# Limiting how far the projection products may run ahead of the score chunks in the PE order of a hybrid encoder kernel

## The chip, the cores and the metric

The kernel runs on one core of a Trainium2 chip. Its metric is the device time of one launch in microseconds (us): the median of repeated executions. One more execution was recorded by the hardware profiler; all views of the profile speak of that one. The engines are named as in the profile: PE (TensorE, matrix products), PEld (its weight loads), DVE (VectorE), ACT (ScalarE), POOL (GpSimd) and SP (SyncE, which here only issues DMAs).

## The reference

Two layers of a bidirectional encoder over 2048 tokens of width 1024. Each layer normalises its input, projects it to the queries, keys, values and gates of four head groups (A: dense attention; B: windowed attention with sinks; C: neighbourhood attention; D: differential attention), joins the four gated outputs and projects back. Cut to what matters here:

```python
for l in range(DEPTH):                       # DEPTH = 2
    h = _rmsnorm(x, norm_g[l])
    z = jnp.einsum('bsd,de->bse', h, w_in[l])          # 1024 -> 3328 columns
    (q_a, k_a, v_a, g_a, q_b, k_b, v_b, g_b,
     q_c, k_c, v_c, g_c, q_d, k_d, v_d, g_d) = jnp.split(z, offs, axis=-1)
    ...
    # group D: 4 query heads, two score maps each, over all 2048 keys
    sc = jnp.einsum('bqkgcd,bskcd->cbkgqs', qi, k).astype(jnp.float32) * scale
    p = jax.nn.softmax(sc, axis=-1)
    w = (p[0] - lam * p[1]).astype(v.dtype)
    o = jnp.einsum('bkgqs,bskd->bqkgd', w, v)
    ...
    x = x + jnp.einsum('bsm,md->bsd', mix, w_out[l])
return _rmsnorm(x, final_g)
```

## The kernel before

A layer has four stages: the D columns are projected (with the transposes of x); then the attention of group D runs while the projections of A, B and C are done in its gaps; then the attention of A runs, with that of B and of C in between; at last the output projection. Precision is kept by splitting each operand of a projection into a high and a low part, so one product of the reference is three matmuls here (lines 320, 322 and 324, `in_proj_k`). The change concerns the second stage, called the D stage below.

**The D stage.** It has 32 units: 2 key heads times 16 tiles of 128 queries. A unit has 16 score chunks. A chunk is a matmul to a PSUM tile S of 128x512 (line 497); DVE copies it to the SBUF tile P and takes its row maximum (line 498). The pool of S has three buffers. After four chunks ACT takes the exponential over 2048 columns (line 505), and after eight DVE combines the two score maps (`comb`, line 724). Then come the unit's 32 transposes of P (tile PTp, line 514, evacuated by ACT at line 475), and the 16 value products (tile O, line 521; the profile shows two records for each). The output of a unit is normalised by a chain that goes through several engines, `fin_d`: the sums of squares by PE (tile fin, line 591), small DVE operations (lines 594, 595, 112), a power on POOL (line 114), DVE again (line 597), the gate on POOL (gg, line 545), and a transpose by PE (fin, line 550).

**The fillers.** The projections of A, B and C are 160 chunks of 24 products each, 3840 products a layer, written as a generator (`filler`) that gives one product of 128x256 at each step. `drive` writes the program of the D stage: it steps through the score chunks, and after each of them `fillers(n)` takes the next products from the generator. A unit has ten slots (two in `gap`, eight fronts), and each slot brings FR2 products. What is left when the first unit of A begins is written in one piece (`switch`).

**What sets the order.** In the D stage the order in which PE, DVE, ACT, POOL and SP issue is not the order in which the program is written. A scheduler goes through the program with a timing model of its own and gives each engine, at each point, the first instruction in program order whose inputs are ready in that model. A product whose score chunk would have to wait is therefore pulled ahead of the chunk. The engines then issue strictly in that order and wait on semaphores. In the stage of A the PE order is the written one (`manual_schedule`).

Of the kernel before, what the change touches and what calls it, by code (L numbers as in the profile page):

```python
# [31 lines left out]
WPT = 13  # L32
WOU = 360
KA0 = 16
FR2 = 11.2
SC64 = 64.0 ** -0.5
SC32 = 32.0 ** -0.5
NEG = -1e30
# [35 lines left out]
def trunk_kernel(ctx, tc, x, norm_g, w_in, w_out, qn_a, kn_a, sink_b, rpb_c, lam_q1, lam_k1, lam_q2, lam_k2,  # L74
                 subln_d, final_g, rope, bmask, out, depth=DEPTH):
    nc = tc.nc
    V, A, G, PE = nc.vector, nc.scalar, nc.gpsimd, nc.tensor
# [181 lines left out]
    for l in range(depth):  # L259
# [93 lines left out]
        with tc.tile_pool(name="wd", bufs=16, reuse_waits="tile") as wp, tc.tile_pool(name="st", bufs=3, reuse_waits="tile") as st:  # L353
# [84 lines left out]
            for t in range(NT):  # L438
                h = hs.pop(t)
                if t == WPT:  # L440
                    wb = big.tile([128, 4, 2, 256], F32R, tag="b", name="wb")
                    for k in range(4):
                        s = st.tile([128, 384], F32, tag="st", name="wst")
# [19 lines left out]
        with tc.tile_pool(name="sm", bufs=6, reuse_waits="tile") as sm, \  # L463
                tc.tile_pool(name="ov", bufs=2, reuse_waits="tile") as ov, tc.tile_pool(name="pp", bufs=2, reuse_waits="tile") as pp, \
                tc.tile_pool(name="sps", bufs=3, space=PSUM, reuse_waits="tile") as sps, tc.tile_pool(name="ops", bufs=1, space=PSUM, reuse_waits="tile") as ops, \
                tc.tile_pool(name="tps2", bufs=2, space=PSUM, reuse_waits="tile") as tps:
            later = []
            vt, kt = {}, {}
            tpool = cycle([tps])

# [9 lines left out]
            def tick():  # L480
                for e in list(later):
                    e[0] -= 1
                    if e[0] <= 0:
                        later.remove(e)
                        e[1]()
# [5 lines left out]
            def dense_scores(q_list, k_ap, scale, nscale, zacc, p):  # L491
                mx = sm.tile([128, 4], F32, tag="mx", name="mx")
                for j in range(4):
                    s = sps.tile([128, 512], F32, tag="s", name="S")
                    c = j * 512
                    for i, q in enumerate(q_list):
                        PE.matmul(s, lhsT=q, rhs=k_ap[:, c:c + 512], start=(i == 0), stop=(i == len(q_list) - 1))  # L497
                    V.tensor_scalar(p[:, c:c + 512], s, 1.0, None, op0=ALU.mult, op1=ALU.max, accum_out=mx[:, j:j + 1])  # L498
                    tick()
                    if j < 3:  # L500
                        yield
                nm = sm.tile([128, 1], F32, tag="nm", name="nm")
                jk = sm.tile([128, 4], F32, tag="jk", name="jk")
                V.tensor_scalar(jk, mx, nscale, None, op0=ALU.mult, op1=ALU.min, accum_out=nm)  # L504
                A.activation(p, p, ACTF.Exp, bias=nm, scale=scale, accum_out=zacc)  # L505
# [114 lines left out]
            def adv(g, n):  # L620
                for _ in range(n):
                    next(g, None)
# [3 lines left out]
            def drive(groups, fill, f_rate, extra):  # L626
# [17 lines left out]
                def fillers(n):  # L644
                    nonlocal fa
                    fa += n
                    k = int(fa)
                    fa -= k
                    adv(fill, k)

                def fin_all():
                    for f in list(fins):
# [3 lines left out]
                def slot(target):  # L656
                    fin_all()
                    n = max(0, math.ceil(target - 1e-6) - cnt[0])
                    for _ in range(n):
                        next(sg, None)  # L660
                        fillers(f_rate / n)
                    if n == 0:
                        fillers(f_rate)

                while cnt[0] < ends[0]:
                    next(sg)
                    fillers(f_rate / 2)
                for k, g in enumerate(groups):
# [8 lines left out]
                    i = 0  # L677
# [50 lines left out]
            if True:  # L728
# [180 lines left out]
                fill = filler()  # L909
# [70 lines left out]
            def a_scores(u):  # L980
                kv, t = u["kv"], u["t"]
                u["pre"]()
                qh, qlo = u["q"]()
                u["g"] = load_gate("A", t, kv)
                zt = sm.tile([128, 2], F32, tag="zt", name="zt")
                u["p"] = pp.tile([128, 2, S], F32, tag="p", name="P")
                for g in range(2):
                    yield from dense_scores([qh[g], qlo[g]], kt["A"][kv], rr_a[:, t, kv * 2 + g:kv * 2 + g + 1],
                                            nrr_a[:, t, kv * 2 + g:kv * 2 + g + 1], zt[:, g:g + 1], u["p"][:, g, :])
                    if g == 0:  # L990
                        yield
                u["rz"] = half_recip(zt)
                yield
# [112 lines left out]
            if True:  # L1106
# [75 lines left out]
                first["s"] = a_first  # L1182
                drive(units_d + [units[i:i + 3] for i in range(0, len(units), 3)], fill, FR2, ex3)
                ph3.close()
# [39 lines left out]
```

## Time and profile before

| What | us |
|---|---|
| median of three runs | 3577.78 |
| lowest and highest of them | 3574.85 and 3580.77 |
| the profiled execution, whole | 3572.38 |
| its span, from first to last instruction | 3570.6 |
| PE busy | 3432.0 |
| DVE busy | 2491.9 |
| ACT busy | 2109.9 |

The profiled execution is 5.4 us below the median, and 1.8 us of it lie outside the span. Of the views used below, the groups give for one line and operation the busy time, the mean duration and the idle time ahead of it; the table by stretches gives, for each stretch of the span (start and end in us, then its length), the busy time and the number of instructions of each engine and the TensorE clock granted; the waits give for whom an engine waited, in total, how often, and the longest; the timeline gives the start, the duration and the instruction. The busy time of PE is modelled: a matmul counts until its modelled end, so a PE that is busy may still be far from its highest rate.

### The profile page before, as it was taken

The numbers are of one execution on the slowest core, as the hardware profiler recorded it, in microseconds if no ns is written. First come the engines' busy times: TensorE is split into PE (matmuls) and PEld (weight loads), VectorE is DVE, ScalarE is ACT, GpSimd is POOL, SyncE is SP. The second block draws the span as 40 slices with busy tenths as digits, with TensorE's granted clock in tenths as the row PEclk, the third lists the DMA queues.
The fourth block names the chain that finished last, engine by engine and source line by source line (L and its number), as shares of the span: only waits on it lengthen the run. The fifth ranks groups of instructions, "written<-read, shape, count | busy, mean of one in ns | idle before, by whom it ended". The sixth has DMA issues, their size and how long they took to land.

```text
span 3570.6 us, 71576 instructions
## 1 busy us (share of the span) xinstructions
PE 3432.0 (96%) x25232; PEld 2964.9 (83%) x25232; DVE 2491.9 (70%) x7827; ACT 2109.9 (59%) x3963; POOL 963.4 (27%) x1604
## 2 busy tenths in 40 slices
PE   8989999999989999999999999999999899899999
PEld 8979889898967777878899888988888678678787
DVE  4387877878878887773234877787778688777733
ACT  4455656556667877771144555665566678777711
POOL 4455432552210001001044553345421000010000
PEclk9999999999999999999999999999999999999999
DMA  4532235323232345335445323252322333543243
GB/s 147 186 107 87 79 80 168 93 83 88 68 101 80 89 115 138 90 101 177 143 137 178 89 79 89 77 177 84 88 79 62 103 85 84 137 115 98 90 159 112
DMA packets 355777, 387.47 MB, mean 109 GB/s; under 512 B 59802, under 2 KB 298586, under 8 KB 350298
## 3 DMA queue, kind: packets, MB, share of 16 engines
q1 hardware_dynamic: 351098, 367.17, 34.8%
q10 hardware_dynamic: 4320, 15.73, 1.3%
q8 instruction: 199, 3.26, 0.4%
q14 instruction: 160, 1.31, 0.1%
HBM read 258.83 MB, written 123.91 MB: 107 GB/s over the span
## 4 chain that ended last, share of the span: by engine, by line
PE 78%; DVE 9%; DMA 4%; ACT 3%; POOL 3%; issue 2%; SPq 1%; DVEq 0%; POOLq 0%; ACTq 0%
PE O L521 11%; PE S L497 10%; PE PTp L514 10%; PE y L218 10%; PE z L320 9%; PE z L324 9%; PE z L322 9%; DVE P L498 4%; PE Obc L540 2%; PE PTp L532 2%; PE Sc L1044 1%; ACT P L505 1%; DMA wst<-in_w_in_dram 1%; DVE wt L314 1%; DVE P L724 1%
## 5 line engine op out<-in xcount | busy, mean ns | idle before, releaser
L498 DVE TENSOR_SCALAR_CACHE_REDUCE P<-S 128x512 f32<-128x512 f32 x1536 | 1025.4, 686 | 260.3 <-PE S L497 205.2
L320 PE MATMUL z<-wt,ht 128*128 128x256 f32 (+1 forms) x3008 | 892.7, 298 | 16.8 <-POOL wt L313 5.5
L322 PE MATMUL z<-wt,ht 128*128 128x256 f32 (+1 forms) x3008 | 887.0, 295 | 0.5 <-DVE wt L314 0.2
L324 PE MATMUL z<-wt,ht 128*128 128x256 f32 (+1 forms) x3008 | 883.1, 294 | 0.0
L514 PE MATMUL PTp<-idr,P 128*128 128x128 f32 x4096 | 630.7, 277 | 36.5 <-ACT P L475 18.2
L475 ACT COPY P<-PTp 128x512 f32<-128x512 f32 x896 | 513.3, 585 | 252.1 <-PE PTp L514 246.8
L505 ACT ACTIVATE P<-P,nm 128x2048 f32<-128x2048 f32 x256 | 514.1, 2008 | 156.6 <-DVE jk L504 153.9
L514 PEld LDWEIGHTS PTp<-idr,P 128*128 128x128 f32 x4096 | 492.2, 143 | 135.8 <-ACT P L475 34.2
L320 PEld LDWEIGHTS z<-wt,ht 128*128 128x128 f32 x3008 | 569.6, 190 | 37.7 <-POOL wt L313 7.3
L322 PEld LDWEIGHTS z<-wt,ht 128*128 128x128 f32 x3008 | 570.7, 190 | 12.5 <-DVE wt L314 2.2
L324 PEld LDWEIGHTS z<-wt,ht 128*128 128x128 f32 x3008 | 570.3, 190 | 9.2 <-issue 1.5
L497 PE MATMUL S<-kA,q 128*128 128x512 f32 x1024 | 361.9, 436 | 0.1
L218 PE MATMUL y<-wot,ms 128*128 128x512 f32 x1440 | 330.8, 392 | 0.0
L218 PEld LDWEIGHTS y<-wot,ms 128*128 128x128 f32 x1440 | 270.8, 188 | 59.7
L545 POOL TENSOR_TENSOR gg<-gt,rzh 128x128 f32<-128x128 f32 x192 | 76.7, 400 | 886.7 <-DVE rzh L606 324.5
L313 POOL TENSOR_SCALAR wt<-wst,g 128x256 fp32r<-128x256 f32 (+1 forms) x336 | 221.0, 669 | 333.3 <-PE z L324 222.1
L724 DVE SCALAR_TENSOR_TENSOR P<-P,cf,P 128x2048 f32<-128x2048 f32 x128 | 307.3, 2401 | 2.2
L505 ACT ACTIVATE P<-P,nm,rr_a 128x2048 f32<-128x2048 f32 x128 | 268.7, 2099 | 62.2 <-DVE jk L504 59.6
L521 PE MATMUL O<-P,vd 128*64 128x256 f32 x2048 | 238.5, 384 | 7.3 <-ACT P L475 7.3
L521 PE MATMUL O<-P,vA 128*64 128x256 f32 x2048 | 235.1, 382 | 0.0
L497 PE MATMUL S<-kd,qd 128*128 128x512 f32 x512 | 209.9, 428 | 9.2 <-DVE P L498 7.6
L497 PE MATMUL S<-kdt,qd 128*128 128x512 f32 x512 | 210.1, 436 | 8.4 <-DVE P L498 5.5
(195 smaller groups left out, 5103.0 us busy)
## 6 DMA issues: line engine op xcount, KB each, us to landing
wst<-in_w_in_dram SPq DMA_DIRECT2D x320, 128.0 KB
qd<-qd SPq DMA_DIRECT2D x128, 128.0 KB
htd<-ht SPq DMA_DIRECT2D x16, 1024.0 KB
ht<-htd SPq DMA_DIRECT2D x16, 1024.0 KB
q<-qsA SPq DMA_DIRECT2D x128, 128.0 KB
q<-qsB SPq DMA_DIRECT2D x64, 256.0 KB
q<-qc SPq DMA_DIRECT2D x64, 256.0 KB
mload<-mx ACTq DMA_DIRECT2D x30, 512.0 KB
```

Source lines behind the costliest of these rows:

```text
L218: PE.matmul(ys[c], lhsT=ms[:, a, kc], rhs=wts[k][:, b, c * 512:(c + 1) * 512], start=(k == 0 and i == 0), stop=(k == KD - 1 and i == 2))
L313: G.tensor_scalar(wt[:, 0, :], s, g8[:, k:k + 1], 0.0, op0=ALU.mult, op1=ALU.add)
L320: PE.matmul(z, lhsT=h[:, 0, kc], rhs=wk[:, 0, :], start=(k == 0), stop=False)
L322: PE.matmul(z, lhsT=h[:, 0, kc], rhs=wk[:, 1, :], start=False, stop=False)
L324: PE.matmul(z, lhsT=h[:, 1, kc], rhs=wk[:, 0, :], start=False, stop=(k == KD - 1))
L475: A.copy(dst, src)
L497: PE.matmul(s, lhsT=q, rhs=k_ap[:, c:c + 512], start=(i == 0), stop=(i == len(q_list) - 1))
L498: V.tensor_scalar(p[:, c:c + 512], s, 1.0, None, op0=ALU.mult, op1=ALU.max, accum_out=mx[:, j:j + 1])
L505: A.activation(p, p, ACTF.Exp, bias=nm, scale=scale, accum_out=zacc)
L514: PE.transpose(tp[:, (h * 2 + a) * 128:(h * 2 + a + 1) * 128], p[:, h, j * 128:(j + 1) * 128], idn)
L521: PE.matmul(u["o"][a * 64:(a + 1) * 64, 0:256], lhsT=u["v"](0, j), rhs=u["p"][:, :, j * 128:(j + 1) * 128], start=(n < 2), stop=(n >= NT - 2))
L724: V.scalar_tensor_tensor(p0, p1, cf, p0, op0=ALU.mult, op1=ALU.add)
```

## The change

Two things change. FR2, the products written per slot, goes from 11.2 to 12.0: ten slots of 12 make 120 products a unit, so the 3840 products of a layer fill 32 units. And every product that `fillers` writes gets an edge to the score chunk sixteen chunks back in the program: the scheduler must place it behind that chunk on PE. The edge carries no semaphore; it only orders instructions of the same engine. Sixteen chunks are one unit.

```diff
-FR2 = 11.2
+FR2 = 12.0
+LAG = 16
...
             later = []
+            score_ins = []
...
-                        PE.matmul(s, lhsT=q, rhs=k_ap[:, c:c + 512], start=(i == 0), stop=(i == len(q_list) - 1))
+                        m = PE.matmul(s, lhsT=q, rhs=k_ap[:, c:c + 512], start=(i == 0), stop=(i == len(q_list) - 1))
+                    score_ins.append(m.ins)
...
                     fa += n
                     k = int(fa)
                     fa -= k
-                    adv(fill, k)
+                    if len(score_ins) > LAG:
+                        with tc.issue_after(score_ins[-1 - LAG]):
+                            adv(fill, k)
+                    else:
+                        adv(fill, k)
```

No instruction is added or removed on any engine: 22274 on PE, 5909 on DVE, 3306 on ACT, 1609 on POOL, 2489 on SP both times. Their order differs from the D stage of each layer on, in the same way in both layers; the PE order of the A stage and of what follows is the same. The lines of the changed kernel are one to seven higher.

Counted in the PE order, between the value products (O) of one unit and of the next stand these numbers of projection products, units 1 to 31 of a layer (the 214 ahead of unit 0's are the same in both):

| Units | before | now |
|---|---|---|
| 1 to 8 | 125 147 138 154 110 96 116 97 | 158 135 176 150 94 102 76 95 |
| 9 to 16 | 125 132 156 166 160 104 118 153 | 164 160 142 128 120 102 115 143 |
| 17 to 24 | 157 140 152 96 117 75 92 124 | 120 120 120 120 96 102 91 77 |
| 25 to 31 | 118 120 151 160 27 0 0 | 115 125 120 178 161 21 0 |

Three places show it. The first is PE behind the value products of unit 29 of the first layer, near the end of the D stage. S is a score chunk, PTp the transposes of P, fin the two steps of the output chain. Before:

```order
L521 MATMUL O<-P,vd 64x256 x16
L514 MATMUL PTp<-idr,P 128x128 x2
L497 MATMUL S<-kdt,qd 128x512 x3
L591 MATMUL fin<-bones,sq 128x2
L514 MATMUL PTp<-idr,P 128x128 x4
L497 MATMUL S<-kdt,qd 128x512 x3
L514 MATMUL PTp<-idr,P 128x128 x8
L497 MATMUL S<-kdt,qd 128x512 x6
L550 MATMUL fin<-idr,gg 128x128
L514 MATMUL PTp<-idr,P 128x128 x16
```

Now:

```order
L524 MATMUL O<-P,vd 64x256 x16
L517 MATMUL PTp<-idr,P 128x128 x2
L321 MATMUL z<-wt,ht_8612 128x256
L323 MATMUL z<-wt,ht_8612 128x256
L325 MATMUL z<-wt,ht_8612 128x256
```

Before, no product is left there (the last one stands 27 products behind the value products of unit 28); now the last 21 products of the layer follow, ahead of the next score chunk.

The second place is PE behind the value products of unit 17, in the middle of the stage. Before (25 products in all stand ahead of the next score chunk):

```order
L521 MATMUL O<-P,vd 64x256 x16
L514 MATMUL PTp<-idr,P 128x128 x2
L324 MATMUL z<-wt,ht_8689 128x256
L320 MATMUL z<-wt,ht_8689 128x256
L322 MATMUL z<-wt,ht_8689 128x256
```

Now:

```order
L524 MATMUL O<-P,vd 64x256 x16
L517 MATMUL PTp<-idr,P 128x128 x2
L499 MATMUL S<-kdt,qd 128x512
L321 MATMUL z<-wt,ht_8277 128x256
L323 MATMUL z<-wt,ht_8277 128x256
L325 MATMUL z<-wt,ht_8277 128x256
```

The score chunk now stands directly behind the transposes, with no product ahead of it; six products and the next chunk follow. The same stands behind the value products of seven units of a layer (12, 13 and 16 to 20); behind those of unit 4 one product and two transposes of queries stand ahead of it as well. Before it stood so only in the part with no products left.

The third place is DVE, in the output chain of unit 21, from the second small operation (line 595 before, 598 now) to the last (597 and 600). L498 and L501 are the evacuations of score chunks, L315 the splitting of projection weights, L778 and L507 small steps of other work. Before:

```order
L594 TENSOR_TENSOR s_11129<-fin,rz_10266 128x2
L595 TENSOR_TENSOR s_11129<-s_11129,rz_10266 128x2
L112 TENSOR_SCALAR dme<-s_11129 128x2
L498 TENSOR_SCALAR P_11074,mx<-S 128x512 x2
L498 TENSOR_SCALAR P,mx<-S 128x512
L597 TENSOR_TENSOR drs<-drs,rz_10266 128x2
```

Now:

```order
L598 TENSOR_TENSOR s_11421<-s_11421,rz_10617 128x2
L501 TENSOR_SCALAR P_11351,mx<-S 128x512
L501 TENSOR_SCALAR P,mx<-S 128x512
L315 SCALAR_TENSOR_TENSOR wt<-wst,g_95,wt 128x256 x2
L778 TENSOR_TENSOR qt<-qT,qt 128x2x128
L113 TENSOR_SCALAR dme<-s_11421 128x2
L315 SCALAR_TENSOR_TENSOR wt<-wst,g_95,wt 128x256
L507 TENSOR_SCALAR jk,nm<-mx 128x4
L501 TENSOR_SCALAR P,mx<-S 128x512
L315 SCALAR_TENSOR_TENSOR wt<-wst,g_95,wt 128x256
L501 TENSOR_SCALAR P,mx<-S 128x512 x2
L600 TENSOR_TENSOR drs<-drs,rz_10617 128x2
```

More DVE work now stands inside this chain; one weight split and one evacuation more stand ahead of the rows shown, behind the chain's first step (line 597). Between the two fin matmuls of that unit PE has 25 products, 9 score chunks and 14 transposes (before 24, 7 and 14), 12 of them of P.

## The prediction

> **What bounds the kernel now.** I read the page first: its totals and the costliest groups.
>
> ```profile
> span 3570.6 us, 71576 instructions
> ...
> PE 3432.0 (96%) x25232; PEld 2964.9 (83%) x25232; DVE 2491.9 (70%) x7827; ACT 2109.9 (59%) x3963; POOL 963.4 (27%) x1604
> ...
> L498 DVE TENSOR_SCALAR_CACHE_REDUCE P<-S 128x512 f32<-128x512 f32 x1536 | 1025.4, 686 | 260.3 <-PE S L497 205.2
> L320 PE MATMUL z<-wt,ht 128*128 128x256 f32 (+1 forms) x3008 | 892.7, 298 | 16.8 <-POOL wt L313 5.5
> ```
>
> PE is busy 96% of the span, and its largest group, the projection products z, hardly ever waits (16.8 us of idle before 3008 of them). DVE's largest group waits mostly for PE. So PE bounds the kernel, and a reordering can win only where PE has too little to do. The table by stretches, cut at the first value product of a unit, shows where that is in the D stage. Columns: stretch, length, PE, PEld, DVE, ACT and POOL busy (instructions), granted clock, DMA.
>
> ```profile
> 831.12:852.73 21.61, 21.61 (x168) 18.74 (x167) 18.31 (x59) 14.88 (x29) 1.10 (x2) 1.00 0.12 32
> 852.73:880.30 27.57, 24.57 (x184) 20.59 (x183) 22.43 (x75) 18.07 (x32) 8.30 (x18) 1.00 0.43 118
> 989.60:1019.89 30.29, 30.29 (x244) 27.99 (x243) 23.12 (x67) 17.90 (x32) 1.45 (x3) 1.00 0.15 42
> 1019.89:1044.54 24.65, 18.42 (x111) 13.41 (x111) 16.90 (x57) 14.98 (x23) 3.72 (x4) 0.86 0.72 173
> 1044.54:1062.92 18.38, 14.95 (x80) 9.51 (x80) 14.19 (x47) 11.06 (x17) 1.09 (x2) 0.91 0.22 76
> 1062.92:1083.71 20.79, 15.80 (x94) 12.08 (x93) 14.86 (x53) 12.60 (x20) 1.09 (x2) 0.84 0.32 101
> ```
>
> The last three stretches are units 29 to 31 of the first layer, 63.8 us together. The same table for the instructions that touch z alone tells why they differ: the products are used up.
>
> ```profile
> 831.12:852.73 21.61, 10.41 (x76) 9.62 (x75) 0.00 (x0) 1.89 (x4) 1.00 0.12 32
> 852.73:880.30 27.57, 12.21 (x92) 11.65 (x92) 0.00 (x0) 1.41 (x3) 1.00 0.43 118
> 989.60:1019.89 30.29, 22.59 (x161) 21.22 (x160) 0.00 (x0) 2.84 (x6) 1.00 0.15 42
> 1019.89:1044.54 24.65, 3.68 (x28) 3.41 (x27) 0.00 (x0) 0.95 (x2) 0.86 0.72 173
> ...
> 231.54:1019.89 788.35, 516.15 (x3599) 478.36 (x3599) 0.00 (x0) 77.87 (x174) 1.00 0.31 90
> 1019.89:1083.71 63.82, 3.68 (x28) 3.41 (x27) 0.00 (x0) 0.95 (x2) 0.87 0.45 121
> 2001.50:2787.99 786.49, 516.70 (x3602) 478.84 (x3602) 0.00 (x0) 78.01 (x174) 1.00 0.31 90
> 2787.99:2850.15 62.16, 3.69 (x28) 3.41 (x27) 0.00 (x0) 0.96 (x2) 0.89 0.46 126
> ```
>
> Units 1 to 28 (788.35 and 786.49 us, the body) hold some 3600 products; units 29 to 31 (the dry end) hold 27 or 28. There PE follows the softmax chain of DVE and ACT, and the waits of the first layer's dry end show on whom (the three groups that matter below):
>
> ```profile
> PE fin L550 <- POOL gg L545: 3.8, 1, 3.8
> PE PTp L514 <- DVE P L724: 2.8, 1, 2.8
> ...
> PE S L497 <- DVE P L498: 1.9, 5, 0.6
> ```
>
> **The change part by part.** The count in the issue order says what moves: by the value products of unit 28, 3658 products have gone by instead of 3813. So 155 leave the body of each layer; 134 go to unit 29 (161 instead of 27) and 21 to unit 30. Two parts, one answer: FR2 alone sets how many are written, the edge keeps the scheduler from pulling more than a unit's worth ahead.
>
> A product's price is the step between starts in a run of products, here the first and the last of a run with 22 steps between them. Below them are a score chunk with its follower, and eight transposes with theirs.
>
> ```profile
> 1024.01 0.28 PE L324 MATMUL z<-wt,ht 128*128 128x256 f32 x1
> ...
> 1026.62 0.28 PE L320 MATMUL z<-wt,ht 128*128 128x256 f32 x1
> ...
> 1007.19 0.39 PE L497 MATMUL S<-kdt,qd 128*128 128x512 f32 x1
> 1007.42 0.28 PE L320 MATMUL z<-wt,ht 128*128 128x256 f32 x1
> ...
> 1011.88 1.04 PE L514 MATMUL PTp<-idr,P 128*128 128x128 f32 x8
> 1012.67 0.47 PE L497 MATMUL S<-kdt,qd 128*128 128x512 f32 x1
> ```
>
> (1026.62 - 1024.01) / 22 = 0.119 us a product; 0.23 a chunk; 0.10 a transpose. The other bound is the difference of two whole units, (30.29 - 21.61) / (161 - 76) = 0.102; I take 0.119, the direct reading.
>
> 1. The body loses 155 x 0.119 = 18.4 us (15.8 by the other price).
> 2. The dry end grows. Unit 29 becomes a full unit like the stretch of 30.29 us (161 products there, 161 here). Unit 30, with 21 products and then the same pattern of chunks and transposes, is taken like the stretch of 24.65 us less 6 products: 23.9. Unit 31 keeps its 20.79. Together 75.0 instead of 63.8: +11.2.
>
> So filling the dry end is worth 18.4 - 11.2 = 7.2 us a layer (4.6 by the lower price), not the whole of the gap, because one dry unit of three is filled and two stay. The second layer's dry end is 1.7 us shorter; I take the same.
>
> 3. New waits for score slots. Seven units now have a chunk directly behind PTp, as only the dry part had before, where it waited:
>
> ```profile
> 1049.12 1.11 PE L497 MATMUL S<-kdt,qd 128*128 128x512 f32 x2 [0.54 <-DVE P L498]
> ```
>
> DVE can begin the next three evacuations only when the value products have freed P, so the fourth chunk waits for the first of them. 7 x 0.54, about 0.2 for unit 4, and less the one that goes from the dry part: +3.5 a layer. Bounds: 0, if the chunk's slot is free earlier, and 8 x 0.6 = 4.8. I take 3.5, the row of the same pattern.
>
> 4. The output chain. While POOL's gate is late, PE stands before the second fin with everything behind it: transposes, chunks, value products. The one such wait, with DVE's chain of that unit and two durations from the body's groups:
>
> ```profile
> 1029.09 0.15 DVE L594 TENSOR_TENSOR s<-fin,rz 128x2 f32<-128x2 f32 x1
> 1037.12 0.15 DVE L597 TENSOR_TENSOR drs<-drs,rz 128x2 f32<-128x2 f32 x1
> ...
> 1037.81 0.47 PE L550 MATMUL fin<-idr,gg 128*128 128x128 f32 x1 [3.79 <-POOL gg L545]
> ...
> L498 DVE TENSOR_SCALAR_CACHE_REDUCE P<-S 128x512 f32<-128x512 f32 x449 | 297.5, 686 | 78.6 <-PE S L497 62.5 <-PE O L521 13.3
> L314 DVE SCALAR_TENSOR_TENSOR wt<-wst,g,wt 128x256 fp32r<-128x256 f32 x144 | 78.8, 577 | 9.8 <-POOL wt L313 9.4
> ```
>
> In the changed order the chain of unit 21 contains six evacuations and five weight splits, 6 x 0.69 + 5 x 0.58 = 7.0 us, and 0.7 more pass from the last DVE step to fin (1037.12 to 1037.81). PE has 25 x 0.119 + 9 x 0.23 + 12 x 0.10 = 6.2 between the two fins: short by 1.5. By the same count unit 5 is short by 1.2, and units 7 and 23 are near balance. PE stops for some of those evacuations in any case, so I take half of 2.7, +1.3 a layer, between 0 and two full waits, 7.6.
>
> 5. Old waits of the body. They are these, first layer (the three smaller groups are left out), 15.1 us:
>
> ```profile
> PE qT L811 <- DVE qc L820: 4.9, 1, 4.9
> PE z L320 <- ACT zv L828: 2.3, 2, 1.7
> PE S L497 <- DVE P L498: 2.2, 7, 0.5
> PE z L320 <- POOL wt L313: 1.7, 2, 1.6
> PE kT L94 <- ACT zkv L779: 1.6, 1, 1.6
> PE O L521 <- ACT P L475: 1.4, 1, 1.4
> PE qT L767 <- POOL qs L761: 1.0, 1, 1.0
> ```
>
> The longest (qT for qc, behind SP's DMAs of C's queries and of the bias table) keeps its neighbours in SP's order. Which of the others stay cannot be read from the old trace; I leave them at 0, with bounds of half of 15.1 less or more, 7.5 either way.
>
> 6. The start of A. Its loads wait on SP behind the last gate stores, and in the changed order the load of vA comes ahead of one B query load. Between the last product and A's first chunk, behind the value products of unit 30, lies now most of one dry stretch (about 20 us of 23.9) instead of most of two (some 40 of 24.65 + 18.38); that still covers a load. I cost it at nothing; uncovered, it would put a wait like the 2.8 us for P in the list above ahead of A's first chunk.
>
> The sum a layer: -7.2 + 3.5 + 1.3 = -2.4; two layers, -5. Against the profiled execution (3572.4) that is 3567; it lies 5.4 below the median of the runs shown, so the median should come to 3577.8 - 5 = 3573.
>
> The clock weighs in here. The granted clock is 0.86, 0.91 and 0.84 in the three dry stretches and 1.00 in the full ones, and the second of them has no wait of even 3 us. The Trainium skill (TensorE: Matmul & The Clock Gate, section Why this matters for your kernels) says that the clock drops after an idle gap of about 3 us on PE. By that rule the dry unit that is filled here would not have slowed, and what it lost to the clock, at most 9% of 18.38 us, 1.7 us, could not be won: the sum would be -2 instead of -5. By the rows the clock also drops in a stretch of many small waits, and the loss goes with the stretch; I keep -5.
>
> **The rivals.**
> - *Old waits go too* (3558). With fewer products pulled ahead, the buffers that the projections share with the transposes are less crowded, and half of the 15.1 us goes in each layer: -5 - 15 = -20. For it: five of the seven waits are of projection work. Against: that work and its order on ACT and POOL change little.
> - *The saving is eaten in thin units* (3585). The two thin stretches above, with 76 and 92 products, differ by 5.96 us, of which 16 products explain 1.9; 4.1 is waits, 2 a thin unit on average. Units of the body with under 105 products are nine now and six before: 3 x 2 x 2 layers = +12, so -5 + 12 = +7, at the edge of what can be told. For it: the thin units lost products too (units 5 to 8: 367 instead of 419). Against: the stretch with the fewest, 76, waits for nothing.
> - *The output chain stops PE in the body* (3601, slower). The mechanism of part 4, at its full price: without products that may be pulled ahead, PE stands 3.79 us at the second fin in units 5, 7, 21 and 23 of both layers: 8 x 3.79 = 30 instead of the 2.6 taken, so -5 + 28 = +23. It decides from 2.4 us a layer more than taken. Against: the body of before shows no such wait in the first layer.
> - *The edge does nothing* (3578): the counts show that PE's order moves, but the time may be set elsewhere.
>
> **How the numbers follow.** My forecast 0.45, alone good for 3563 to 3583; old waits go 0.22; thin units 0.16; output chain 0.13; nothing 0.04. A measurement of this kernel tells some 0.2%, 7.2 us, from no change: below 3570.6 is faster, above 3584.9 slower. Of the forecast 0.19 lies below that edge: faster is 0.19 + 0.21 = 0.40. Same: 0.26 + 0.01 + 0.08 (half of the thin units) + 0.04 = 0.39. Slower: 0.08 + 0.13 = 0.21. The range 3554 to 3592 leaves out a third of the first rival (0.07) and most of the third (0.10).
>
> **What would show it.** In the changed profile, cut at the value products: units 29, 30 and 31 take about 30, 24 and 21 us; the body is 12 to 15 us shorter than 788; PE's waits for P at S rise from 2.2 to about 6 us in the body; waits of 1 to 2 us at fin for gg appear in units 5 and 21. The prediction is wrong if the dry end is longer than 80 us, if fin waits for gg over 6 us in the body (the slower rival), or if the body's other waits move by more than 7 us a layer.

## The result and the profile after

| | before | after |
|---|---|---|
| median of the timed runs, us | 3579.07 | 3556.27 |
| lowest and highest, us | 3574.85 and 3580.77 | 3553.45 and 3560.75 |
| the profiled execution, us | 3572.38 | 3557.79 |
| its span, us | 3570.6 | 3556.0 |
| both D stages, from unit 0's value products to unit 31's, us | 1700.8 | 1682.9 |

The ratio is 0.994, with a 95% interval of 0.9928 to 0.9952: 22.8 us faster. The forecast was 3573, 5 us faster, in a range of 3554 to 3592. The direction and the range held, the range by 2.3 us; the gain is over four times what the sum gave. Two medians further down, those of the rate alone and of the edge with 11.7, each contain one far slower run (4237.92 and 3622.39 us); without it they are 3567.73 and 3553.19, and the ratios leave it out.

The totals and two groups of the page of after:

```profile
span 3556.0 us, 71545 instructions
...
PE 3423.5 (96%) x25232; PEld 2960.4 (83%) x25232; DVE 2493.2 (70%) x7827; ACT 2106.1 (59%) x3963; POOL 940.8 (26%) x1604
...
L501 DVE TENSOR_SCALAR_CACHE_REDUCE P<-S 128x512 f32<-128x512 f32 x1536 | 1025.1, 686 | 233.7 <-PE S L499 164.1
L321 PE MATMUL z<-wt,ht 128*128 128x256 f32 (+1 forms) x3008 | 894.1, 298 | 15.4 <-ACT ht L171 4.9
```

The work is the same, and so are its durations (686 ns an evacuation, 298 ns a product). What differs is how long PE stands and how fast it runs. The table by stretches, cut as in the prediction: the body of the first layer, its units 29, 30 and 31, then body and dry end of the second layer. Columns as there.

```profile
234.09:1001.50 767.41, 750.44 (x5871) 672.64 (x5870) 612.01 (x1862) 469.46 (x807) 291.90 (x513) 1.00 0.31 92
1001.50:1031.87 30.37, 30.37 (x245) 28.09 (x245) 22.82 (x68) 18.27 (x33) 2.16 (x4) 1.00 0.15 45
1031.87:1056.04 24.17, 17.97 (x103) 12.39 (x102) 16.28 (x57) 14.70 (x23) 3.72 (x4) 0.83 0.77 202
1056.04:1074.65 18.61, 15.93 (x94) 11.01 (x93) 12.32 (x44) 10.47 (x18) 1.09 (x2) 0.85 0.46 133
1995.04:2765.64 770.60, 750.74 (x5871) 672.96 (x5870) 611.69 (x1861) 470.01 (x807) 291.95 (x512) 1.00 0.31 91
2765.64:2837.38 71.74, 63.19 (x439) 50.95 (x439) 51.41 (x168) 43.44 (x73) 6.97 (x10) 0.90 0.42 122
```

The same for the instructions that touch z: 3444 products in the body instead of 3599, 161 in unit 29, 21 in unit 30.

```profile
234.09:1001.50 767.41, 494.30 (x3444) 460.31 (x3444) 0.00 (x0) 75.11 (x168) 1.00 0.31 92
1001.50:1031.87 30.37, 22.97 (x162) 21.44 (x161) 0.00 (x0) 3.05 (x7) 1.00 0.15 45
1031.87:1056.04 24.17, 2.81 (x22) 2.56 (x21) 0.00 (x0) 0.71 (x2) 0.83 0.77 202
```

The body became 20.9 us shorter in the first layer and 15.9 in the second; the dry ends became 9.3 and 9.6 longer. The four numbers sum to -17.9. That is more than the 14.6 us between the two spans, because the rest of the program was longer in this execution: the stretch ahead of the first unit alone by 2.6 us (234.09 against 231.54).

Whom PE waited for, first the body of the first layer, then its dry end (total, times, longest, in us):

```profile
PE S L499 <- DVE P L501: 8.0, 12, 1.4
PE PTp L517 <- ACT P L477: 4.3, 3, 3.7
PE O L524 <- ACT P L477: 1.9, 1, 1.9
PE z L321 <- DVE qt L778: 1.5, 1, 1.5
...
PE fin L553 <- POOL gg L548: 3.8, 1, 3.8
PE PTp L517 <- ACT P L477: 1.7, 2, 1.4
```

Against the lists of before, first layer: the waits for score slots rose from 2.2 to 8.0 us; the waits of qT for qc and for qs, of kT for zkv, of z for zv and for wt are gone (in the second layer 1.0 us of z for zv stays); waits of PTp and O for ACT took part of their place; the wait of PTp for the combination (DVE P, line 724 before) is gone from the dry end, and its 3.8 us at fin stayed. Three readings from the timeline of PE say what these are:

```profile
397.11 0.50 PE L499 MATMUL S<-kd,qd 128*128 128x512 f32 x1 [1.21 <-DVE P L501]
...
605.28 0.50 PE L499 MATMUL S<-kd,qd 128*128 128x512 f32 x1 [1.39 <-DVE P L501]
...
742.12 0.50 PE L499 MATMUL S<-kdt,qd 128*128 128x512 f32 x1 [1.02 <-DVE P L501]
...
830.48 0.51 PE L499 MATMUL S<-kdt,qd 128*128 128x512 f32 x1 [0.90 <-DVE P L501]
831.48 1.11 PE L499 MATMUL S<-kdt,qd 128*128 128x512 f32 x2 [0.50 <-DVE P L501]
832.64 0.33 PE L553 MATMUL fin<-idr,gg 128*128 128x128 f32 x1
```

The rows at 605 and 742 are the two longest waits of the seven places where a chunk now stands directly behind PTp; the seven waits there are 0.43, 1.39, 0.54, 0.54, 1.02, 0.54 and 0.43, 4.9 us. The rows at 397 and at 830 and 831 stand between the two fin matmuls of units 5 and 21, and the last row shows that fin itself then has nothing to wait for.

The third reading is the wait of 4.91 us that qT had for qc in unit 9 of before. Here are ACT and PE of after at the same point of the program (its unit 8), behind the row of ACT of before:

```profile
458.26 0.27 ACT L819 CAST qc<-qT 128x128 fp32r<-128x128 f32 x1 [9.23 <-DMA qc<-qc]
...
452.99 0.27 ACT L826 CAST qc<-qT 128x128 fp32r<-128x128 f32 x1 [4.42 <-DMA qc<-qc]
453.15 0.59 ACT L477 COPY P<-PTp 128x512 f32<-128x512 f32 x1
...
453.80 0.96 PE L517 MATMUL PTp<-idr,P 128*128 128x128 f32 x4 [3.65 <-ACT P L477]
```

In both kernels ACT stands at the cast of qc until a DMA of C's queries has landed, and PE stands for what is behind it on ACT: first a transpose of queries, now the transposes of P. It is one wait under two names. Here it is 1.3 us shorter; in the second layer it is 2.2 us before and 3.8 after, so its size changes from one layer and execution to the next.

### The profile page after: what moved, and what is told of

Same layout as the page of the kernel before. It is cut to its first block, busy times and chain, and to the rows that moved or that the text cites. A ratio compares the mean times of both kernels' runs of the same rounds, so it can differ in the third digit from the quotient of the medians.

```text
span 3556.0 us, 71545 instructions
## 1 busy us (share of the span) xinstructions
PE 3423.5 (96%) x25232; PEld 2960.4 (83%) x25232; DVE 2493.2 (70%) x7827; ACT 2106.1 (59%) x3963; POOL 940.8 (26%) x1604
## 4 chain that ended last, share of the span: by engine, by line
PE 45%; DVE 4%; DMA 2%; ACT 2%; issue 1%; POOL 1%; SPq 0%; DVEq 0%; ACTq 0%; POOLq 0%
PE y L219 10%; PE O L524 6%; PE S L499 5%; PE PTp L517 5%; PE z L321 5%; PE z L323 5%; PE z L325 5%; DVE P L501 2%; PE Obc L543 1%; PE PTp L535 1%; PE Sc L1051 1%; DVE wt L315 1%; ACT P L508 1%; DMA wos<-in_w_out_dram 0%; DMA wst<-in_w_in_dram 0%
## 5 line engine op out<-in xcount | busy, mean ns | idle before, releaser
L501 DVE TENSOR_SCALAR_CACHE_REDUCE P<-S 128x512 f32<-128x512 f32 x1536 | 1025.1, 686 | 233.7 <-PE S L499 164.1
L314 POOL TENSOR_SCALAR wt<-wst,g 128x256 fp32r<-128x256 f32 (+1 forms) x336 | 206.9, 626 | 383.4 <-PE z L325 237.8
```

The lines of the kernel that those rows point to most:

```text
L314: G.tensor_scalar(wt[:, 0, :], s, g8[:, k:k + 1], 0.0, op0=ALU.mult, op1=ALU.add)
```

## The experiments

Three theories. **A**: the gain is what the prediction's steps 1 and 2 say, products taken out of full units and put into dry ones; other terms are small. **B**: the cap itself makes the body less crowded, whatever the dry end. **C**: the body's waits differ by some us a layer with every change of the order, without a rule that either A or B gives. All edits below are against the changed kernel, and all times are compared with the kernel before, run on the same chip beside them.

**1. The rate alone.** The edge is never applied.

```diff
-LAG = 16
+LAG = 100000
```

> FR2 = 12.0 as in the changed kernel, but the edge is never applied (LAG = 100000). Counted in its PE order, the products end even earlier than before: behind the value products of units 27 to 30 stand 32, 0, 0 and 0 of them, one dry unit more than before (27, 0, 0). Theory A (the time follows the dry end: a unit without products leaves PE idle for 7 to 10 us, and what is taken out of the body is paid at 0.119 us a product): one more dry unit, +7 us a layer, +14 us in all, 3593 us. Theory B (the time follows the edge: without products pulled far ahead the buffers shared by projections and transposes are less crowded and the body waits less): no edge, so as before, 3579 us.

Measured: 3568.33 against 3578.32, ratio 0.9974 (0.9964 to 0.9984). Without the edge the products are used up a unit earlier (32 in unit 28, none behind), so the dry end is four units; A asked for a loss, and there is none. Body and dry end of the first layer in this kernel:

```profile
229.27:1018.36 789.09, 775.39 (x6052) 696.06 (x6051) 616.95 (x1870) 475.75 (x822) 300.46 (x516) 0.99 0.33 94
1018.36:1077.94 59.58, 47.08 (x259) 32.74 (x258) 48.04 (x161) 38.70 (x58) 3.30 (x6) 0.86 0.27 85
```

The D stages are 1699.5 us, 1.4 less than before. Each layer has one more dry unit, unit 28, which the cut counts with the body. The named waits of that longer body fell from 16.0 to 12.1 us in the first layer (qT for qc, 4.9 us, is now a wait of z for qc of 2.0) and hardly moved in the second (13.2 and 13.6), and units 29 to 31 are 3 to 4 us shorter. Why the longer dry end costs nothing here stays open. So the rate by itself saves next to nothing in the D stages, and A and B both missed the time. Of the timed difference of 10 us the profiles place 4 to 7 outside the D stages (1865.4 us in this execution, 1869.8 and 1872.5 in the two of before); why is not shown.

**2. The edge alone, 11.2 products a slot.**

```diff
-FR2 = 12.0
+FR2 = 11.2
```

> FR2 = 11.2 as before, with the edge to the score chunk sixteen back. In its PE order the last three units hold 141, 174 and 96 products: there is no dry end. A score chunk stands directly behind the value products' transposes in 13 units instead of the changed kernel's 8. Theory A: the dry end's idle time (23 us a layer before, 17 to 19 in the changed kernel) goes almost wholly, the waits for score slots cost 0.6 us in each of 13 units, 7 a layer: -15 us a layer, 3549 us. Theory B: the same edge as the changed kernel, so its time, 3556 us.

Measured: 3560.58 against 3578.32, ratio 0.995 (0.9933 to 0.9966). The edge carries the gain. Units 29, 30 and 31 have 141, 174 and 96 products, so no unit is dry; the waits show what was paid for it:

```profile
PE S L499 <- DVE P L501: 10.8, 19, 1.7
...
PE S L499 <- DMA q<-qsA: 2.6, 1, 2.6
...
PE kT L95 <- DMA kl<-ksB: 1.2, 1, 1.2
```

The first row is the body (14.9 us in the second layer), the others are units 29 to 31. Score slots cost 9 to 13 us a layer more than before, and the loads at the start of A, which the prediction's step 6 says are covered while a dry unit lies ahead of them, are now waited for: 3.8 us. A's forecast of 3549 had 7 us a layer for the score slots, and nothing for the loads.

**3. The edge with 12.8 products a slot**, so that the dry end is long in spite of the edge.

```diff
-FR2 = 12.0
+FR2 = 12.8
```

> The edge to the chunk sixteen back as in the changed kernel, but FR2 = 12.8: the products are written sooner, and in the PE order they end in unit 28 (54 products, then none in units 29 to 31). Theory A: a dry end of three whole units and part of a fourth, some 28 us idle a layer against 23 before, and 3 waits for score slots: +6 us a layer, 3591 us. Theory B: the edge is there, so as the changed kernel, 3556 us.

Measured: 3594.60 against 3578.32, ratio 1.0044 (1.0029 to 1.0059). B falls: the edge is the same as in the changed kernel, and the body is not less crowded (waits of qT for zkv of 3.0 us and of PTp for mix of 2.1 stand in its full units). A's 3591 is nearly met, but not by A's reason. Units 29 to 31 have as few products as in experiment 1 and take as long (59.76 against 59.58 us); the 15 us a layer between the two kernels stand in the body (804.46 against 789.09), where the named waits are 20.9 instead of 12.1 us. So the length of the dry end alone does not set the time, and the order of the body can cost more than the whole change gains. The clock of its dry end comes up again below.

```profile
229.92:1034.38 804.46, 781.65 (x6055) 697.49 (x6054) 615.29 (x1878) 478.43 (x824) 297.07 (x516) 0.99 0.32 92
1034.38:1094.14 59.76, 48.41 (x256) 30.58 (x257) 47.28 (x154) 36.72 (x56) 3.29 (x6) 0.89 0.29 83
...
PE PTp L517 <- ACT P L477: 2.9, 3, 1.7
PE PTp L517 <- DVE P L731: 2.5, 2, 1.4
```

**4. The edge with 11.5.**

```diff
-FR2 = 12.0
+FR2 = 11.5
```

> The edge as in the changed kernel and FR2 = 11.5: in the PE order units 29 to 31 hold 179, 167 and 14 products, so only the last is dry; 7 units have the score chunk directly behind the transposes, as in the changed kernel. Theory A: of the dry end's 23 us a layer about 5 are left, the score slots cost 4: -14 us a layer, 3550 us. Theory B: as the changed kernel, 3556 us. If the loads for the stage of A are no longer covered (they wait for the last product), its first score chunk waits and the gain is smaller by that wait.

Measured: 3547.87 against 3578.32, ratio 0.9914 (0.9899 to 0.9929), as A said. No D unit is dry but the last (179, 167 and 14 products), and the whole dry end has one wait left, the load of B's keys at the start of A:

```profile
PE kT L95 <- DMA kl<-ksB: 4.2, 1, 4.2
```

**5 and 6. The edge in one part of the stage only.** In the first sixteen units, with 12.0:

```diff
-                    if len(score_ins) > LAG:
-                        with tc.issue_after(score_ins[-1 - LAG]):
+                    lag = LAG
+                    if LAG < len(score_ins) <= 256:
+                        with tc.issue_after(score_ins[-1 - lag]):
```

> FR2 = 12.0, with the edge for the first 256 score chunks of a layer only (units 0 to 15). In the PE order units 1 to 13 hold the same products as in the changed kernel, and units 24 to 31 the same as before the change (124 118 120 151 160 27 0 0): the old dry end with the new first half. Theory A (the dry end sets what is won, a product moved is paid at 0.119 us, and a score slot that waits costs 0.6 us): nothing won, two more score slots wait, 3580 us. Theory B (the edge wins in the body): half the body has it, so half of the gain or more, 3567 us or less. A third possibility, C, after the run with FR2 = 12.0 alone, which was 10 us faster with a longer dry end: the waits of the body differ from order to order by up to 8 us a layer either way; then the time lies within 16 us of 3578 and the trace shows it in the body's waits.

From unit 20 on, in the last twelve units, with 11.2 and a reach that goes from 54 chunks down to 32 (the short name "second half" below means this run):

```diff
-FR2 = 12.0
+FR2 = 11.2
...
-                    if len(score_ins) > LAG:
-                        with tc.issue_after(score_ins[-1 - LAG]):
+                    lag = max(32, 54 - (len(score_ins) - 320) // 4)
+                    if len(score_ins) > 320:
+                        with tc.issue_after(score_ins[-1 - lag]):
```

> FR2 = 11.2 as before and the edge only from score chunk 321 of a layer on (unit 20), first at a distance of 54 chunks, then falling to 32. In the PE order units 0 to 16 hold the same products as before the change, and the last three 171, 99 and 0: the old first half with a dry end of one unit, behind which the loads of A are covered. Theory A: the dry end's idle time falls from 23 to about 6 us a layer, four score slots wait (2 us): -15 us a layer, 3548 us. Theory B: the edge stands in the last third only, a third of the changed kernel's gain, 3570 us. Theory C: as A, with up to 8 us a layer either way in the body's waits, 3532 to 3564 us.

Measured: 3572.22 against 3579.02, ratio 0.9982 (0.9972 to 0.9991), for the first half; 3558.28, ratio 0.9939 (0.9924 to 0.9953), for the second. The first half leaves the dry end as it was before (27 products in unit 29); what it does to the body is worth 1 to 4 us a layer. The second run alone, with its lower rate and longer reach, gives what the whole change gives. The body of the first layer in the one, and the waits of the body in the other:

```profile
231.96:1016.44 784.48, 769.29 (x6026) 689.87 (x6025) 618.39 (x1874) 475.48 (x820) 292.36 (x514) 1.00 0.32 91
...
PE S L499 <- DVE P L501: 7.0, 15, 1.0
PE qT L819 <- DVE qc L828: 5.4, 1, 5.4
```

The second row keeps the old wait of qT for qc, which the changed kernel has at PTp: what sets its name is the order of the first half, where C's queries are projected. A's and B's numbers missed in both runs; C's bounds held, but they are wide.

**7. The edge with 11.7, and 8, the kernel before once more**, unchanged, for a second profile.

```diff
-FR2 = 12.0
+FR2 = 11.7
```

> The edge as in the changed kernel and FR2 = 11.7: in the PE order units 28 to 31 hold 149, 164, 98 and 0 products: one dry unit, whose length covers the loads of A (with FR2 = 11.5, 14 products in the last unit, the first of them waited 4.2 us). Theory A: the dry end's idle time falls from 23 to about 6 us a layer, score slots wait in 8 units (5 us): -12 us a layer, 3554 us, a little slower than FR2 = 11.5 in the score slots and without its wait of 4 us: 3546 to 3554 us. Theory B: as the changed kernel, 3556 us.

> The kernel before, once more, for a second profile: how far the single waits of the body and the first stage differ between executions of one and the same order. The two layers of the first profile differ by 2 us in the body (788.4 and 786.5 us), mostly in one wait of 4.9 and 2.2 us. Expected: the same waits, each within 3 us, and a span of 3570 to 3578 us.

Measured: 3553.57 against 3579.02, ratio 0.9928 (0.9908 to 0.9948), with the 11.7; the profile's D stages are 1676.5, 24 less than before, with no wait for gg in the dry end. Before again: 3575.34, D stages 1701.0 against 1700.8 in the first profile, and the same waits (qT for qc 5.4 us in place of 4.9). Over the D stages these two executions agree within 0.2 us, though single waits differ by up to 2.4 us (that wait was 4.9 and 5.4 in the first layer, 2.2 and 4.6 in the second).

**9. The changed kernel once more**, unchanged.

> The changed kernel once more, on the same chip as the three below, for a second profile and a second ratio. Between the first profiles of the two kernels the span differs by 14.6 us, between the medians of their timed runs by 22.8 us. If the difference of the timed runs is real and the profiles are at the ends of their scatter, this run is again 20 to 25 us below the kernel before and its span lies below 3556; if the medians were off, it is some 15 us below.

Measured: 3554.26 against 3578.73, ratio 0.9934 (0.9913 to 0.9954). The gain is real, 24.5 us here. The D stages are 1679.1, 21.9 us less than in the second profile of before and 3.8 less than in the first of after. The groups of waits are nearly those shown above; in unit 5, though, PE stands 1.07 us at fin for gg, where the first profile has 1.21 at S.

**10. A shorter reach**, eight chunks.

```diff
-LAG = 16
+LAG = 8
```

> FR2 = 12.0 as in the changed kernel, with the edge eight chunks back instead of sixteen. In the PE order units 28 to 31 hold 158, 139, 66 and 0 products: 43 more than the changed kernel's 139 come from the body into the dry end, which then is one unit and a half; the score chunk stands directly behind the transposes in 10 units instead of 8. Theory A: the dry end's idle time falls from 17 to about 7 us a layer, score slots cost 2 us more, so -8 us a layer against the changed kernel, 3540 us; with the body's waits growing by 5 us a layer as the products that covered them leave (seen in the runs with FR2 = 11.7 and with the edge in the second half), 3550 us. Theory B (a tighter edge, a better body): the body's idle time falls below 27 us a layer.

Measured: 3558.11 against 3578.73, ratio 0.9941 (0.9925 to 0.9957). A asked for 3540 to 3550 and missed. The dry end is better, as A said (139 and 66 products in units 29 and 30), but the body pays:

```profile
232.91:1006.56 773.65, 751.54 (x5848) 671.41 (x5847) 614.57 (x1860) 467.17 (x806) 291.10 (x509) 1.00 0.31 90
1006.56:1073.72 67.16, 60.18 (x462) 51.38 (x461) 51.90 (x169) 43.71 (x75) 8.39 (x14) 1.00 0.47 128
...
PE S L499 <- DVE P L501: 9.0, 16, 2.4
PE S L499 <- DMA wst<-in_w_in_dram: 2.5, 1, 2.5
PE PTp L517 <- DVE s L597: 2.5, 1, 2.5
```

**11 and 12. Two versions meant to be faster**, 11.6 with a reach of 24, and 11.8 with 16.

```diff
-FR2 = 12.0
-LAG = 16
+FR2 = 11.6
+LAG = 24
```

> A try for the best version: FR2 = 11.6 and the edge 24 chunks back. In the PE order units 28 to 31 hold 168, 140, 52 and 0 products, and 6 units have the score chunk directly behind the transposes (fewer than with 16). Theory A: dry end 7 us idle a layer, body about 30 as before the change, since the products may still run one unit and a half ahead to cover its waits: 37 instead of 54 us, -33 us in all, 3546 us. If the cap's distance does not matter for the body (35 us as with FR2 = 11.7 and 16 chunks), 3555 us.

```diff
-FR2 = 12.0
+FR2 = 11.8
```

> FR2 = 11.8 and the edge 16 chunks back. In the PE order units 28 to 31 hold 176, 139, 53 and 0 products, and 7 units have the score chunk directly behind the transposes. It stands between the changed kernel (12.0: 178, 161, 21, 0) and 11.7 (149, 164, 98, 0). Theory A: dry end 7 to 8 us idle a layer (17 in the changed kernel, 3.5 with 11.7), body 27 to 35: 3546 to 3560 us.

Measured: 3546.87, ratio 0.9906 (0.9876 to 0.9937), as A said, and 3537.38, ratio 0.9884 (0.9852 to 0.9915), both against 3578.73. The last is the fastest kernel seen, 41 us under the one before and about 18 under the changed one; it was one of several orders run, and the lucky one among neighbours. Its D stages are 15.5 and 11.7 us under those of the two profiles of the changed kernel; the rest of the 18 lies outside them. Its first layer, body and then units 29, 30 and 31, and the first of the waits of the body:

```profile
231.26:997.25 765.99, 749.69 (x5861) 670.87 (x5861) 612.55 (x1861) 469.95 (x806) 305.11 (x510) 1.00 0.32 92
...
997.24:1026.82 29.58, 28.01 (x223) 25.58 (x222) 23.19 (x67) 17.97 (x31) 3.87 (x7) 1.00 0.16 43
1026.82:1049.07 22.25, 19.72 (x134) 15.91 (x133) 15.88 (x54) 13.66 (x24) 3.64 (x4) 0.92 0.45 140
1049.07:1066.22 17.15, 13.30 (x93) 9.78 (x93) 13.29 (x47) 12.31 (x20) 1.10 (x2) 1.00 0.92 242
...
PE S L499 <- DVE P L501: 3.7, 9, 0.5
```

Unit 30 has 53 products here and takes 22.25 us; the changed kernel's has 21 and takes 24.17. Gone are the wait of 3.8 us at fin for gg and most of the slow clock behind it. DVE's order says why the wait is gone: the gate's last input no longer stands behind the combination. The last operation of the output chain (line 600) and the combination (line 731) in the changed kernel, and then in this one:

```profile
1046.49 2.35 DVE L731 SCALAR_TENSOR_TENSOR P<-P,cf,P 128x2048 f32<-128x2048 f32 x1
1048.76 0.15 DVE L600 TENSOR_TENSOR drs<-drs,rz 128x2 f32<-128x2 f32 x1
...
1038.17 0.16 DVE L600 TENSOR_TENSOR drs<-drs,rz 128x2 f32<-128x2 f32 x1
...
1042.55 2.35 DVE L731 SCALAR_TENSOR_TENSOR P<-P,cf,P 128x2048 f32<-128x2048 f32 x1
```

All kernels side by side. The products are counted in the order; the dry end is units 29 to 31, both layers together; S is PE's wait for score slots in the two bodies; the D stages hold the same work in every row, so their differences are how long PE stands and how fast it runs. In the rows of the rate alone and of 12.8 the products end in unit 28 (32 and 54 of them), which counts with the body.

| Kernel | products in units 29, 30, 31 | dry ends | S | D stages | median |
|---|---|---|---|---|---|
| before | 27, 0, 0 | 126.0 | 4.2 | 1700.8 | 3579.07 |
| rate alone, 12.0 | 0, 0, 0 | 118.6 | 4.6 | 1699.5 | 3568.33 |
| edge 16, 12.8 | 0, 0, 0 | 117.9 | 8.3 | 1725.9 | 3594.60 |
| edge in the first half | 27, 0, 0 | 125.4 | 9.5 | 1695.3 | 3572.22 |
| after: edge 16, 12.0 | 161, 21, 0 | 144.9 | 17.1 | 1682.9 | 3556.27 |
| edge 16, 11.8 | 139, 53, 0 | 136.5 | 6.9 | 1667.4 | 3537.38 |
| edge 24, 11.6 | 140, 52, 0 | 136.3 | 19.0 | 1675.8 | 3546.87 |
| edge 8, 12.0 | 139, 66, 0 | 134.4 | 18.6 | 1683.3 | 3558.11 |
| edge 16, 11.7 | 164, 98, 0 | 146.5 | 15.3 | 1676.5 | 3553.57 |
| edge in the second half, 11.2 | 171, 99, 0 | 147.6 | 13.6 | 1681.0 | 3558.28 |
| edge 16, 11.5 | 179, 167, 14 | 172.3 | 11.1 | 1676.9 | 3547.87 |
| edge 16, 11.2 | 141, 174, 96 | 182.7 | 25.7 | 1685.5 | 3560.58 |

The rows fall into two groups. The four kernels with at most 27 products in units 29 to 31 have D stages of 1695.3 to 1725.9 us, the eight with 182 or more 1667.4 to 1685.5. That is the evidence across orders for products in the dry units; inside each group the number of products does not sort the times.

## Why the prediction was right, and where its sum was not

The direction and the mechanism held: PE's products were moved out of full units into dry ones, and the profile shows them there. The size did not: -2.4 us a layer was the sum, and the D stages give -9.9, the mean of both layers in two executions of each kernel. That the time still lies in the range was luck: 3556 is outside the 3563 to 3583 for which the forecast's own working was called good, and the range reaches down to 3554 only for the rival *Old waits go too*, whose reason the runs do not bear out. Step by step, with those means:

| Step | forecast, us a layer | measured |
|---|---|---|
| 1. products leave the body | -18.4 | -18.4, taken: 155 of them, as counted |
| 2. the dry end grows | +11.2 | +9.6 (62.5 to 72.1) |
| 3 and 4. score slots and the output chain | +4.8 | +5.9, all of it at S |
| 5. old waits of the body | 0 | -4.1 (13.4 to 9.3) |
| nothing named | 0 | -2.9 |
| sum | -2.4 | -9.9 |

1. The count held (3599 to 3444). The body became 19.5 us shorter, and that is this step, the waits below and 2.9 us that no named wait explains. The price of a product is not at fault: with the edge and 11.2 the first layer's body has 384 products fewer than before and, less its named waits, is 44.1 us shorter ((788.35 - 16.0) - (750.89 - 22.6)), 0.115 us a product, and by the same sum 0.118 in the second layer. So the 2.9 stay open.

2. Unit 29 took 30.37 us (30 was the forecast) and unit 30 24.17 (23.9). The step failed at "Unit 31 keeps its 20.79": it took 18.61, and 17.16 in the second execution. A unit without products has no fixed length. In the kernel before, PTp waited 2.8 us in it for the combination, and that wait is gone. In the runs with 11.8 and with the edge from unit 20 on such a unit takes 17.15 us, at a clock of 1.00.

3 and 4. The pattern of step 3, a chunk directly behind PTp, holds at all seven places, at 4.9 us instead of 7 x 0.54 = 3.8, since two of the seven waits are of 1.0 and 1.4 us. Step 4's shortfalls were worked out as 1.2 us in unit 5 and 1.5 in unit 21. They are there, at 1.21 and at 0.90 + 0.50, but under the name of S: the evacuations that delay the chain delay the chunks ahead of fin first, and once PE has waited for those, gg is there. In the second execution unit 5 has its wait at fin instead, 1.07 us, and unit 21 has 0.66 at S. Halving the shortfalls was too low in both executions, and looking for them at fin alone was wrong. The slower rival on the output chain falls with this: not one wait of 3.8 us at fin stands in the body. What step 3 left out is that some old waits at S go, which is why 4.9 + 2.6 stands beside +5.9.

5. This is the step that failed in kind: new waits were added at their full price and the old ones left at 0. The largest part of what the sum missed lies here, before the 2.9 of no name and the 1.6 of step 2. But *Old waits go too*, whose 3558 is nearest to the time, had another reason and another size: half of 15.1 us, because fewer products are pulled ahead and buffers are less crowded. It was 4.1, and experiment 3 has the same edge and waits as long as before in its full units (S aside, 13.5 us in units 1 to 27 of the first layer, against 13.8 in the body of before). What the rows show is a change of neighbours: the longest old wait went on under another name (4.91 at qT, 3.65 at PTp), because its cause, a DMA of C's queries that ACT waits for, was not touched; the waits of z and kT for ACT and POOL are nearly all gone in this order, and in others they are there again (kT for zkv 1.6 with the edge in the first half, z for wt 1.6 with the edge in the second). That is theory C. No run here gives a rule for them. The rival of the thin units falls: nine of them stand in the body, and it came out 2.9 us a layer shorter than its named terms, not 6 longer (of the 4.1 us that this rival called waits, the trace of before names 2.7). The rival that the edge does nothing falls with the interval of the ratio.

6. The start of A was covered, as forecast: no DMA is named among PE's waits from unit 29 to the first chunks of A. The price of its being uncovered was put at about 2.8 us; with products in every dry unit it measured 3.8 and 4.2.

The clock. The prediction kept -5 against the -2 that a rule of the Trainium skill gives (TensorE: Matmul & The Clock Gate, section Why this matters for your kernels: the clock drops after a gap of about 3 us). The filled unit runs at 1.00, and the next at 0.83 in its place; over the whole dry end of the first layer the clock was 0.87 and 0.92 in the two executions of before and 0.91 and 0.90 in those of after, in the second layer 0.89 in both before and 0.90 in both after. So the loss moved on rather than going, and the gain of this change is not one of clock. In the changed kernel the slow stretch does come with a wait of 3.8 us at fin, as the rule has it; in experiment 3 the dry end ran at 0.89 with no wait above 1.7 us, which the rule does not explain.

That the D stages show -17.9 and -21.9 in profiles and the medians -22.8 and -24.5 leaves 3 to 5 us that are not placed; the stretches outside the D stages differ by as much between two executions of one kernel (unit 0's value products begin at 231.2 and at 234.1 us in the two of after).

## What to carry to other kernels

When filler work runs out ahead of the work that it fills, price both ends: a piece moved saves its own length in the full stretch and costs less than that in a thin one (here 18.4 us saved and 9.6 paid for 155 pieces). What a thin unit takes does not follow from its number of pieces alone: it took 24.17 us with 21 of them and, in another order, 22.25 with 53. Do not add new waits and leave the old ones standing: in a fixed order a long wait covers, or is renamed by, the next one, so follow the cause (here a DMA that ACT stood for) and not the instruction that is shown waiting. Neighbouring values of one knob give unrelated orders (11.7, 11.8 and 12.0 lie within 19 us and not in sequence), so time several rather than argue for one.

## What the runs showed of the hardware

The granted clock was lost in pieces of one size. Here are two stretches of the body of after, around the waits at 453.80 and at 830, and two neighbouring products inside the first of them:

```profile
830.00:838.00 8.00, 6.91 (x37) 6.10 (x38) 7.30 (x22) 5.30 (x8) 0.70 (x2) 0.79 0.42 114
452.00:458.00 6.00, 4.20 (x19) 3.01 (x21) 3.58 (x14) 3.51 (x9) 2.46 (x10) 0.72 0.52 138
...
834.01 0.41 PE L321 MATMUL z<-wt,ht 128*128 128x256 f32 x1
834.23 0.41 PE L323 MATMUL z<-wt,ht 128*128 128x256 f32 x1
```

Inside each the granted clock is 0.50 (from 833.0 to 836.0 us, and from 454.2 to 457.3). At that half speed the slow part is 2 x 0.21 x 8 = 3.4 us in the one and 2 x 0.28 x 6 = 3.4 us in the other; from 833.8 to 836.1 the products start about 0.21 us apart instead of 0.12. The piece at 833 followed waits of only 0.90 and 0.50 us. The dry ends of after lost about four such pieces each (2 x 0.09 x 73.15 = 13.2 us in the first layer). The Trainium skill (TensorE: Matmul & The Clock Gate, Part 1) gives a window of about 3.4 us that runs freely; the traces agree with that length. By these starts a piece costs a stretch full of products about 1.5 us (an estimate, 3.4 x (1 - 0.12/0.21)). A stretch that waits anyway can lose little by it: unit 30 of the changed kernel took 24.17 us at a clock of 0.83 in one execution and 24.15 at 0.77 in the other. In the dry ends of the first layer the mean clock was 0.87 and 0.92 before, 0.91 and 0.90 after, 0.98 with 11.8 and 1.00 with the shorter reach: the kernels with 53 and 66 products in unit 30 kept it, the one with 21 did not, and the fastest kernel is among those that did. The shares of clock and waits in its gain were not taken apart.
